# A hybrid decoder trunk on one core: the front and the RG-LRU gates in another order

## The chip, the cores and the metric

The kernel runs on one NeuronCore of a Trainium2 chip. TensorE does the matrix products, VectorE, ScalarE and GpSimd the elementwise work, and the SyncE queue most of the transfers. The traces call them PE, DVE, ACT, POOL and SP. The metric is the device time of one execution in microseconds (us); lower is better.

## The reference, cut to what matters

Two decoder layers over one sequence of 1024 tokens with 1024 features. Layer 0 joins native sparse attention with a second head group whose keys an indexer chooses: for each query, the 256 keys with the highest score. Layer 1 joins an RG-LRU (a width-4 convolution and a gated linear recurrence) with an mLSTM. Around each stand an RMSNorm, a gated side input and residual adds.

```python
hn = rmsnorm(x, norm_g[i])
# layer 0, the indexer: 4 heads of 64
idx_score = einsum('bqh,bqhs->bqs', wi, relu(einsum('bqhd,bsd->bqhs', qi, b_ki)))
_, sel_b = lax.top_k(where(key_pos <= t, idx_score, NEG), 256)
# layer 1, the RG-LRU: 8 blocks of 64
xc = causal_dwconv(x, conv_w, conv_b)
r  = sigmoid(einsum('bsgi,gij->bsgj', xb, wa) + ba)
ig = sigmoid(einsum('bsgi,gij->bsgj', xb, wx) + bx)
a  = exp(-8 * r * softplus(-lam))
h  = scan(a, sqrt(1 - a*a) * (ig * xc))
```

## The kernel before

A program in a tile language whose scheduler sets the order of instructions on each engine, except where a call goes through `Pinned`, which keeps the written order among the pinned calls of that engine.

Products are made in three passes (`mm3`): weights and activations are split into a high part (a ScalarE copy) and a low part (the rest, a subtraction on VectorE or GpSimd), and high × high, high × low and low × high are summed. The helper is `split`; in the trace its two lines are L119 (ScalarE) and L120 (VectorE or GpSimd).

*Front.* `x` is loaded in two halves of 512 tokens, eight tiles of 128 features (index `k`) each. `scaled` (L170, L171) multiplies by the norm's weights and splits, `square_sum` (L127, L130) sums squares, and `norms` turns the sum into 1/rms through a matmul (`ps_ss`, L139), a root, small VectorE steps and a broadcasting matmul (`ps_rs`, L160). The weights `wb` of the token-major projection are loaded beside `x` and split to `wbx` (k 0 to 5) and `wb` (k 6 and 7). For each of eight tiles of 128 tokens, 24 matmuls of 348 columns (8 k by three passes) make `ps_tok`. Tiles 0 to 3 are of half 0, 4 to 7 of half 1.

*Indexer.* `proj` (three passes over 8 k and two halves, 48 matmuls of 512 columns) makes the index queries and keys from chunks `wa[0]` to `wa[2]`. Then for query tiles 2 to 7 and four heads `ps_idx` goes through a ScalarE `relu` and a VectorE multiply-add (L363, L365) into `xall`.

*Search.* The 256th score of each query is found bit by bit, 31 steps. In each, VectorE makes `cand`, VectorE and ScalarE count (ScalarE into `junka`), and VectorE decides (`keep`, `pre`). Meanwhile TensorE makes sixteen projections (chunks 7 to 22), whose weights are loaded two chunks ahead by `fetched` (two loads from GpSimd's queue, then two `part` calls: ScalarE's `wh`, GpSimd's `wl`). A round is one chunk with two or three search steps. Each result goes through VectorE (`qz`). After the last round VectorE chooses the keys, makes `kc` and `blk`, and TensorE goes on with `ps_hid` (L542).

*RG-LRU.* For each of four chunks: a projection, its convolution (`conv`: VectorE `cin`, ScalarE, three VectorE steps into `lru`), a split to `xh` and `xl`, 12 gate matmuls (`ps_g`) with their sigmoids and the scan, and two more projections (chunks 4+c and 8+c, the mLSTM's q and k) whose convolutions end in `qk`. Then the mLSTM starts with `ps_S` (L1146).

Of the kernel before, what the change touches and what calls it, by code (L numbers as in the profile page):

```python
# [20 lines left out]
KT = 8  # L21
# [19 lines left out]
def rd(ap):  # L41
    return ap.bitcast(F32)
# [15 lines left out]
def trunk_kernel(ctx: ExitStack, tc: tile.TileContext, a, out):  # L58
    nc = tc.nc
    T, V, A, G = nc.tensor, nc.vector, nc.scalar, nc.gpsimd  # L60

    const = ctx.enter_context(tc.tile_pool(name="const", bufs=1))
    wq = nc.gpsimd
# [6 lines left out]
    def tmp(dt=F32, name="tmp", shape=(128, 512)):  # L70
        return tmpp.tile(list(shape), dt, name=name, tag="tmp")
# [4 lines left out]
    def mm1(name="mm1"):  # L76
        return psum.tile([128, 512], F32, name=name, tag="m1", bufs=3)

    def mmn(name):
        return psum.tile([128, 512], F32, name=name, tag="n1", bufs=1)  # L80
# [14 lines left out]
    rel = enter("rel", bufs=4)  # L95
    bigp = enter("big", bufs=7)
    wts, stage = enter("wts", bufs=3), 3
# [3 lines left out]
    def big(dt=F32, name="big", shape=(128, 1024)):  # L101
        return bigp.tile(list(shape), dt, name=name, tag="big")
# [7 lines left out]
    gn = const.tile([128, 3, KT], F32, name="gn")  # L110
# [7 lines left out]
    def split(h, l, src, eng=V):  # L118
        A.activation(h, src, AF.Copy)  # L119
        eng.tensor_tensor(l, src, rd(h), op=OP.subtract)  # L120
# [3 lines left out]
    def square_sum(x, acc):  # L124

        sq = tmp(name="sq")[:, :x.shape[1]]
        A.activation(sq, x, AF.Square)  # L127
        if acc is None:
            return sq
        V.tensor_tensor(sq, acc, sq, OP.add)  # L130
        return sq
# [36 lines left out]
    def scaled(x, g, k, h, l):  # L168

        A.activation(h, x, AF.Copy, scale=gn[:, g, k:k + 1])  # L170
        V.scalar_tensor_tensor(l, x, gn[:, g, k:k + 1], rd(h), op0=OP.mult, op1=OP.subtract)  # L171

    def norms(acc, cols, rows, i, table=False, later=0):
        c = rstd(acc, table)
        V.tensor_copy(cols[:, i * 4:i * 4 + 4], c)
        with tc.high_priority(offset=-later):
            A.activation(rows[:, HALF[i]], along(c), AF.Copy)
# [18 lines left out]
    def proj(src, X, nk=KT, w=None):  # L196
        w = w or weights(src, (nk, 128))
        ps = mm2("ps_proj")
        for c, sl in enumerate(HALF):
            for k in range(nk):  # L200
                mm3(ps[:, sl], *w[k], *X[c][k], k == 0, k == nk - 1)
        return ps
# [15 lines left out]
    def stack_q(ps, dst):  # L218
        for sl, t in times_norm(ps):
            for e in range(2):  # L220
                own, oth = slice(e * 64, e * 64 + 64), slice(64 - e * 64, 128 - e * 64)
                A.activation(dst[e][own, sl], t[own], AF.Copy)
                V.tensor_tensor(dst[e][oth, sl], t[own], rd(dst[e][own, sl]), OP.subtract)
# [8 lines left out]
    def stack_hl(t, own, k):  # L232
        oth = slice(64 - own.start, 128 - own.start)
        A.activation(k[own], t[own], AF.Copy)
        V.tensor_tensor(k[oth], t[own], rd(k[own]), OP.subtract)
# [6 lines left out]
    wb = []  # L242
# [4 lines left out]
    xin, win = [], []  # L247
# [19 lines left out]
    load_wb(big(name="wb"), 2)  # L267
    for k in range(0, KT, 2):
        load_x(1, k)
    for i in range(2):  # L270
        for k in range(KT):
            if i == 0:
                b = wbx[:, k * 696:k * 696 + 696] if k < 6 else big(F32R, "wb")
                wb.append((b[:, :348], b[:, 348:696]))
                split(*wb[k], win[k], G)
            scaled(xin[4 * i + k // 2][:, k % 2], 0, k, *X[i][k])
        acc = None
        for k in range(KT):
            acc = square_sum(xin[4 * i + k // 2][:, k % 2], acc)
        norms([acc], ncol, nrow, i, True)  # L280


    tok = l0.tile([128, NT, 348], F32, name="tok")
# [48 lines left out]
    qi = []  # L332
    for c in range(2):
        q2 = pair(n=("qi", "qi"))
        stack_q(proj(a["wa"][c], X), q2)
        qi += q2
    ps = proj(a["wa"][2], X)
    ki, kb = pair(), key()
    for sl, t in times_norm(ps):
        stack_k(t, lo, ki[0][:, sl], ki[1][:, sl])  # L340
        stack_hl(t, hi, kb[:, sl])


    xall = xp.tile([128, 4224], F32, name="xall", tag="x")
# [3 lines left out]
    for t in range(2, NT):  # L348
        n = 128 * (t + 1)
        xs[t] = xall[:, 64 * t * (t + 1) - 384:64 * t * (t + 1) - 384 + n]  # L350
        ms[t] = mall[:, 64 * t * (t + 1) - 384:64 * t * (t + 1) - 384 + n]
        for h in range(4):
            for c in range(0, n, 512):
                m = min(512, n - c)
                ps = mm1("ps_idx")
                for i in range(2):
                    T.matmul(ps[:, :m], qi[h][:, t * 128:(t + 1) * 128], ki[i][:, c:c + m], start=i == 0, stop=i == 1)
                x = xs[t][:, c:c + m]
                e = V
                r = rel.tile([128, 512], F32, name="relu", tag="relu")  # L360
                A.activation(r[:, :m], ps[:, :m], AF.Relu)
                if h == 0:
                    e.tensor_scalar(x, r[:, :m], wi[:, t, 0:1], None, op0=OP.mult)  # L363
                else:
                    e.scalar_tensor_tensor(x, r[:, :m], wi[:, t, h:h + 1], x, op0=OP.mult, op1=OP.add)  # L365
        V.tensor_tensor(xs[t][:, n - 128:], xs[t][:, n - 128:], cst0[:, C_CM - C_W:C_CM - C_W + 128], OP.add)


# [20 lines left out]
    junka = xp.tile([128, 1024], mybir.dt.int8, name="junka")  # L389
    bigc = const.tile([128, 1], F32, name="bigc")  # L390
    V.memset(bigc, BIG)
    PV, PA = Pinned(tc, V), Pinned(tc, A)

    def count(x, thresh, op, dst):
        PV.tensor_scalar(junk[:, :x.shape[1]], x, thresh, None, op0=op, op1=OP.add, accum_out=dst)
# [47 lines left out]
            mm3(ps, *w[k], *X[i][k], k == 0, k == KT - 1)  # L443
        V.tensor_tensor(out, ps, nrow[:, HALF[i]], OP.mult)

    def fetched(c):

        wh, wl = (wts.tile([128, 1024], F32R, name=n, tag=n) for n in ("wh", "wl"))
        parts = []
        for i in range(2):  # L450
            sl = slice(i * 512, i * 512 + 512)
            w = wts.tile([128, 512], F32, name="w", tag="w", bufs=stage)
            wq.dma_start(w.rearrange("p (a b) -> p a b", b=128), a["wa"][c][:, i * 4:i * 4 + 4])

            def part(w=w, sl=sl):
                PA.activation(wh[:, sl], w, AF.Copy)
                G.tensor_tensor(wl[:, sl], w, rd(wh[:, sl]), op=OP.subtract)  # L457
            parts.append(part)
        return [(wh[:, k * 128:k * 128 + 128], wl[:, k * 128:k * 128 + 128]) for k in range(KT)], parts

    def q_done(c, t):
        q2 = pair(n=("qst", "qst"))
        PA.activation(q2[0], t, AF.Copy)
# [8 lines left out]
        count(xs[t], 0.0, OP.is_ge, cnt[:, t - 2:t - 1])  # L472
    PV.tensor_scalar(pre, cnt, 255.5, -1.0, op0=OP.is_lt, op1=OP.mult)
    bits = list(range(30, -1, -1))
    chunks = list(range(7, 23)) + [3, 4, 6, 5]
    ends = [[2], [7], [6], [5], [4, 3]]
    got = [fetched(chunks[0]), fetched(chunks[1])]
    for _, parts in got:
        for f in parts:
            f()  # L480
    todo = []
    for n, c in enumerate(chunks[:16]):
        ps = proj(None, X, w=got[n][0])
# [80 lines left out]
    def first_keys(w, dst):  # L564
        ps, t = mm2("ps_kw")[:, :512], small.tile([128, 512], F32, name="kwp", tag="bt")
        half_proj(ps, w, 0, t)
        keys_of_groups(t, dst, HALF[0])

    def prefetch(c):
        w, parts = fetched(c)  # L570
        for f in parts:
            f()
        return w

    ps = proj(None, X, w=got[16][0])
    wkw = prefetch(6)
# [518 lines left out]
    for c in range(4):  # L1095

        ps = proj(a["ra"][c], X)
        late = []
        for half, sl in enumerate(HALF):
            conv(ps, c, half, x[:, sl])  # L1100
            xh, xl = rec(F32R, "xh"), rec(F32R, "xl")
            split(xh, xl, x[:, sl])
            pg = [mm1("ps_g"), mm1("ps_g")]
            for i in range(2):
                mm3(pg[i], *gws[i * 4 + c], xh, xl, True, True)
            A.activation(r[:, sl], pg[0], AF.Sigmoid, bias=vec[:, 0, c:c + 1])
            late.append(pg[1])
        for half, sl in enumerate(HALF):
            A.activation(ig[:, sl], late[half], AF.Tanh, scale=0.5, bias=vec[:, 1, c:c + 1])
            V.scalar_tensor_tensor(x[:, sl], ig[:, sl], 1.0, x[:, sl], op0=OP.add, op1=OP.mult)  # L1110
        h = hs[c]
        A.activation(ig, r, AF.Tanh, scale=s8[:, c:c + 1])
        A.activation(r, r, AF.Exp, scale=s8[:, c:c + 1])
        A.activation(h, r, AF.Square)
        V.scalar_tensor_tensor(h, h, 1.0, ig, op0=OP.add, op1=OP.mult)
        A.activation(h, h, AF.Sqrt, scale=-0.25)
        V.tensor_tensor(x, x, h, OP.mult)
        V.tensor_tensor_scan(h, r, x, 0.0, op0=OP.mult, op1=OP.add)
        v = wide(h1, (128, 2, S), F32, "qk")
        for i in range(2):  # L1120
            ps = proj(a["ra"][4 + 4 * i + c], X)
            for half, sl in enumerate(HALF):
                y = conv(ps, 4 + 4 * i + c, half, tmp(name="conv"))
                o = v[:, i, sl]
                A.activation(o, y, AF.Tanh, scale=0.5)
                V.scalar_tensor_tensor(o, o, 1.0, y, op0=OP.add, op1=OP.mult)
            qk[4 * i + c] = v[:, i]
# [203 lines left out]
```

## Time and profile before

| | |
|---|---|
| Three runs | 1558.91, 1560.05, 1555.63 us (median 1558.91) |
| The profiled execution | 1555.86 us; its span from first to last instruction is 1553.8 |
| TensorE busy | 1485.8 us (96%), mean granted clock 0.983 |
| VectorE, ScalarE, GpSimd busy | 1004.5 (65%), 799.8 (51%), 507.2 us (33%) |

A busy TensorE isn't one at its peak: its matmuls are pipelined and their shown ends overlap the next starts, so its pace is read from the distance between starts. "Granted clock" is the share of 2.4 GHz that the chip granted TensorE.

### The profile page before, as it was taken

How to read it: one execution, taken by the hardware profiler on the slowest of the kernel's cores; microseconds unless marked ns; L12 is line 12 of the kernel's file. 1: busy time of each engine (PE TensorE's matmuls, PEld its weight loads, DVE VectorE, ACT ScalarE, POOL GpSimd, SP SyncE). 2: the span in 40 equal slices, each digit the busy share in tenths (PEclk: the TensorE clock that was granted, in tenths of full speed). 3: DMA queues.
4: the chain of work that ended last, by engine and by line, in shares of the span. 5: the costliest groups of instructions: out<-in, count | busy, mean ns of one | idle time of the engine just before them, and what ended most of it. 6: DMA issues, size and time to landing. Idle time of an engine off the chain costs nothing.

```text
span 1553.8 us, 23978 instructions
## 1 busy us (share of the span) xinstructions
PE 1485.8 (96%) x8608; PEld 1226.2 (79%) x8608; DVE 1004.5 (65%) x2464; ACT 799.8 (51%) x1667; POOL 507.2 (33%) x506
## 2 busy tenths in 40 slices
PE   6999999998899999999999999999999999999996
PEld 5866888876677888888888789877777888788785
DVE  6269888975679888886234555287776654434456
ACT  6357878325678888777223335356654432223311
POOL 4204552312344453443232412022211122223636
PEclk9999999999999999999999999999999999999998
DMA  5402552255332121200323322011110021222203
GB/s 184 113 9 79 140 141 88 109 169 140 96 82 63 43 68 36 55 23 2 123 89 100 107 79 81 14 42 41 48 34 28 28 81 43 70 93 82 81 1 109
DMA packets 78088, 117.23 MB, mean 75 GB/s; under 512 B 7616, under 2 KB 43073, under 8 KB 77969
## 3 DMA queue, kind: packets, MB, share of 16 engines
q1 hardware_dynamic: 71360, 99.42, 21.1%
q0 software_dynamic: 3952, 12.62, 2.6%
q10 hardware_dynamic: 2656, 3.66, 1.0%
q8 instruction: 68, 1.11, 0.3%
q14 instruction: 52, 0.42, 0.1%
HBM read 94.83 MB, written 24.13 MB: 77 GB/s over the span
## 4 chain that ended last, share of the span: by engine, by line
PE 63%; DVE 17%; ACT 10%; issue 5%; POOL 2%; DMA 2%; SPq 0%; DVEq 0%; ACTq 0%; POOLq 0%
PE ps_proj L192 9%; PE ps_proj L193 9%; PE ps_proj L194 9%; PE ps_s L614 5%; PE ps_o L654 5%; ACT junka L53 5%; PE ps_pt L641 4%; PE ps_gate L192 3%; PE ps_gate L193 3%; PE ps_gate L194 3%; DVE L L622 3%; DVE tk L53 2%; DVE qz L53 1%; DVE conv L1082 1%; DVE lru L1082 1%
## 5 line engine op out<-in xcount | busy, mean ns | idle before, releaser
L120 POOL TENSOR_TENSOR wl<-w,wh 128x512 fp32r<-128x512 f32 (+1 forms) x110 | 155.7, 1432 | 463.3 <-ACT wh L119 445.5
L119 ACT ACTIVATE wh<-w 128x512 fp32r<-128x512 f32 (+1 forms) x110 | 64.8, 620 | 206.3 <-PE ps_proj L193 166.5
L626 ACT ACTIVATE L<-L,st 128x640 f32<-128x640 f32 (+7 forms) x192 | 143.1, 746 | 33.9 <-DVE st L622 26.2
L192 PE MATMUL ps_proj<-x1n,wh 128*128 128x512 f32 x384 | 152.0, 396 | 0.0
L614 PE MATMUL ps_s<-key,q 128*128 128x256 f32 (+3 forms) x576 | 150.5, 368 | 1.2 <-DVE st L622 0.6
L194 PE MATMUL ps_proj<-x1n,wl 128*128 128x512 f32 x384 | 151.4, 394 | 0.0
L193 PE MATMUL ps_proj<-x1n,wh 128*128 128x512 f32 x384 | 151.1, 394 | 0.0
L643 ACT ACTIVATE pt<-ps_pt 128x512 f32<-128x512 f32 (+3 forms) x288 | 124.4, 465 | 37.2 <-PE ps_pt L641 27.1
L192 PE MATMUL ps_proj<-x,wh 128*128 128x512 f32 x336 | 133.5, 397 | 1.8 <-ACT wh L53 1.8
L193 PE MATMUL ps_proj<-x,wh 128*128 128x512 f32 x336 | 134.3, 400 | 0.0
L194 PE MATMUL ps_proj<-x,wl 128*128 128x512 f32 x336 | 132.6, 395 | 1.7 <-POOL wl L457 1.7
L641 PE MATMUL ps_pt<-cst,L 128*128 128x128 f32 x816 | 125.6, 277 | 5.3 <-DVE L L631 4.3
L654 PE MATMUL ps_o<-pt,tok 128*64 128x128 f32 x1632 | 121.9, 281 | 0.6 <-ACT pt L643 0.6
L614 PEld LDWEIGHTS ps_s<-key,q 128*128 128x128 f32 x576 | 94.8, 193 | 24.3 <-issue 10.4
L641 PEld LDWEIGHTS ps_pt<-cst,L 128*128 128x128 f32 x816 | 95.3, 141 | 18.6 <-issue 5.5
L654 PEld LDWEIGHTS ps_o<-pt,tok 128*64 128x64 f32 x1632 | 91.9, 137 | 22.8 <-issue 18.5
L457 POOL TENSOR_TENSOR wl<-w,wh 128x512 fp32r<-128x512 f32 x40 | 54.2, 1363 | 149.4 <-ACT wh L53 149.3
L53 ACT ACTIVATE junka<-xall,cand 128x384 int8<-128x384 f32 (+2 forms) x93 | 83.6, 899 | 25.3 <-DVE cand L53 23.3
L193 PE MATMUL ps_proj<-y,wh 128*128 128x512 f32 x240 | 93.5, 389 | 0.8 <-DVE y L120 0.8
L192 PE MATMUL ps_proj<-y,wh 128*128 128x512 f32 x240 | 93.5, 389 | 0.1
L194 PE MATMUL ps_proj<-y,wl 128*128 128x512 f32 x240 | 93.4, 389 | 0.0
L53 DVE TENSOR_SCALAR_CACHE_REDUCE junk<-xall,cand 128x512 bf16<-128x512 f32 (+2 forms) x93 | 85.9, 924 | 3.3
(426 smaller groups left out, 3635.2 us busy)
## 6 DMA issues: line engine op xcount, KB each, us to landing
q<-qd SPq DMA_DIRECT2D x64, 256.0 KB, 4.1
w<-in_ra_dram SPq DMA_DIRECT2D x48, 256.0 KB, 2.6
w<-in_wa_dram POOLq DMA_DIRECT2D x46, 256.0 KB, 3.0
qd<-qst SPq DMA_DIRECT2D x32, 256.0 KB, 3.2
w<-in_wo_dram SPq DMA_DIRECT2D x32, 256.0 KB, 2.8
w<-in_gatew_dram SPq DMA_DIRECT2D x32, 256.0 KB, 2.9
x<-in_x_dram SPq DMA_DIRECT2D x8, 512.0 KB, 9.5
zd<-qz SPq DMA_DIRECT2D x8, 512.0 KB, 2.6
```

The costliest lines, as they stand in the source:

```text
L53: return self.tc.keep_in_program_order(getattr(self.eng, name)(*args, **kw))
L119: A.activation(h, src, AF.Copy)
L120: eng.tensor_tensor(l, src, rd(h), op=OP.subtract)
L192: T.matmul(ps, wh, xh, start=first, stop=False)
L193: T.matmul(ps, wh, xl, start=False, stop=False)
L194: T.matmul(ps, wl, xh, start=False, stop=last)
L457: G.tensor_tensor(wl[:, sl], w, rd(wh[:, sl]), op=OP.subtract)
L614: T.matmul(s[:, :m], q[:, i, h, :], keys[:, k0 + c:k0 + c + m], start=i == 0, stop=i == 1)
L626: A.activation(L[:, :n], L[:, :n], AF.Exp, bias=prev, scale=-1.0, accum_out=st[:, 2:3])
L641: T.transpose(pt[:, i * 128:(i + 1) * 128], L[:, (b + i) * 128:(b + i + 1) * 128], ident)
L643: A.activation(p[:, :m * 128], pt[:, :m * 128], AF.Copy)
L654: T.matmul(O[(h % 2) * 64:(h % 2) * 64 + 64, c * 128:c * 128 + 128], tok[:, d["k0"] // 128 + i, vi * 64:vi * 64 + 64], ps[i], start=False, ...
```

## The change

Three edits. In the front, TensorE begins with 14 products on a tile of zeros; half 0 is scaled and `wb` is split first, in a pinned order of ScalarE, VectorE and GpSimd, and squares come after that, those of half 0 between the scaling of half 1, those of half 1 last. The weights of the three index projections are fetched and split with pinned calls too, and the first two chunks of the search are fetched before the scores and split between them, one `part` after each of tiles 2 to 5. In the RG-LRU the next projection (chunk 4+c) is written ahead of the first half's gates.

```diff
-    for i in range(2):
-        for k in range(KT):
-            if i == 0:
-                b = wbx[:, k * 696:k * 696 + 696] if k < 6 else big(F32R, "wb")
-                wb.append((b[:, :348], b[:, 348:696]))
-                split(*wb[k], win[k], G)
-            scaled(xin[4 * i + k // 2][:, k % 2], 0, k, *X[i][k])
-        acc = None
-        for k in range(KT):
-            acc = square_sum(xin[4 * i + k // 2][:, k % 2], acc)
-        norms([acc], ncol, nrow, i, True)
+    idle = rel.tile([128, 512], BF, name="idle", tag="relu")
+    V.memset(idle, 0.0)
+    ps = mmn("ps_idle")
+    for _ in range(WARM):
+        T.matmul(ps, idle[:, :128], idle, start=True, stop=True)
+    PV, PA, PG = Pinned(tc, V), Pinned(tc, A), Pinned(tc, G)
...
+    def scale_tile(i, k):
+        h, l = X[i][k]
+        PA.activation(h, part(i, k), AF.Copy, scale=gn[:, 0, k:k + 1])
+        PV.scalar_tensor_tensor(l, part(i, k), gn[:, 0, k:k + 1], rd(h), op0=OP.mult, op1=OP.subtract)
+
+    def square(i, k, acc):
+        sq = tmp(name="sq")
+        PA.activation(sq, part(i, k), AF.Square)
+        if acc is not None:
+            PV.tensor_tensor(sq, acc, sq, OP.add)
+        return sq
+
+    for k in range(KT):
+        b = wbx[:, k * 696:k * 696 + 696] if k < 6 else big(F32R, "wb")
+        wb.append((b[:, :348], b[:, 348:696]))
+        PA.activation(wb[k][0], win[k], AF.Copy)
+        PG.tensor_tensor(wb[k][1], win[k], rd(wb[k][0]), op=OP.subtract)
+        scale_tile(0, k)
+    acc = None
+    for k in range(KT):
+        acc = square(0, k, acc)
+        scale_tile(1, k)
+    norms([acc], ncol, nrow, 0, True)
+    acc = None
+    for k in range(KT):
+        acc = square(1, k, acc)
+    norms([acc], ncol, nrow, 1, True)
...
+            PG.dma_start(w.rearrange("p (a b) -> p a b", b=128), a["wa"][c][:, i * 4:i * 4 + 4])
+
+            def part(w=w, sl=sl):
+                PA.activation(wh[:, sl], w, AF.Copy)
+                PG.tensor_tensor(wl[:, sl], w, rd(wh[:, sl]), op=OP.subtract)
...
+    wi3 = [prefetch(c) for c in range(3)]
...
-        stack_q(proj(a["wa"][c], X), q2)
+        stack_q(proj(None, X, w=wi3[c]), q2)
...
-    ps = proj(a["wa"][2], X)
+    ps = proj(None, X, w=wi3[2])
...
+    chunks = list(range(7, 23)) + [3, 4, 6, 5]
+    got = [fetched(chunks[0])]
+    ready = got[0][1][:]
...
+        if ready:
+            ready.pop(0)()
+            if not ready and len(got) == 1:
+                got.append(fetched(chunks[1]))
+                ready = got[1][1][:]
...
-    got = [fetched(chunks[0]), fetched(chunks[1])]
-    for _, parts in got:
-        for f in parts:
-            f()
...
+            if half == 0:
+                ahead = proj(a["ra"][4 + c], X)
...
-            ps = proj(a["ra"][4 + 4 * i + c], X)
+            ps = proj(a["ra"][8 + c], X) if i else ahead
```

On ScalarE in the front (high parts `x_102` to `x_105` are half 0, `x_106` and on half 1), before:

```order
L170 ACTIVATE x_103<-x,gn 128x512 x2
L119 ACTIVATE wbx<-wb 128x348 x2
L127 ACTIVATE sq<-x 128x512
L170 ACTIVATE x_104<-x,gn 128x512 x2
L119 ACTIVATE wbx<-wb 128x348 x2
L127 ACTIVATE sq<-x 128x512
L170 ACTIVATE x_105<-x,gn 128x512 x2
L127 ACTIVATE sq<-x 128x512 x4
L170 ACTIVATE x_106<-x,gn 128x512 x2
L119 ACTIVATE wb<-wb 128x348 x2
```

And of the change, from the fourth weight on (a pinned call's line is L54):

```order
L54 ACTIVATE wbx<-wb 128x348
L54 ACTIVATE x_103<-x,gn 128x512
L54 ACTIVATE wbx<-wb 128x348
L54 ACTIVATE x_104<-x,gn 128x512
L54 ACTIVATE wbx<-wb 128x348
L54 ACTIVATE x_104<-x,gn 128x512
L54 ACTIVATE wb<-wb 128x348
L54 ACTIVATE x_105<-x,gn 128x512
L54 ACTIVATE wb<-wb 128x348
L54 ACTIVATE x_105<-x,gn 128x512
L54 ACTIVATE sq<-x 128x512
L54 ACTIVATE x_106<-x,gn 128x512
```

The last two weight copies (`wb`, k 6 and 7) no longer stand behind six squares and two copies of half 1.

On GpSimd in the search, one round before (`DMA` issues one half of a chunk's load, `wl` is a half's low part, `qst` that of a query result):

```order
L464 TENSOR_TENSOR qst<-qz,qst 128x1024
L457 TENSOR_TENSOR wl<-w,wh 128x512
L453 DMA w<-in_wa_dram 128x512
L457 TENSOR_TENSOR wl<-w,wh 128x512
L453 DMA w<-in_wa_dram 128x512
```

And of the change:

```order
L506 TENSOR_TENSOR qst<-qz,qst 128x1024
L54 TENSOR_TENSOR wl<-w,wh 128x512 x2
L54 DMA w<-in_wa_dram 128x512 x2
L506 TENSOR_TENSOR qst<-qz,qst 128x1024
L54 TENSOR_TENSOR wl<-w,wh 128x512 x2
```

The first load of a chunk is issued one low part later, together with the second.

On TensorE at the second RG-LRU chunk's gates, before (row numbers count a kernel's rows on the engine; of the next projection's 48 matmuls 23 stand ahead of the first gate matmul):

```order
3576 L192 MATMUL ps_proj<-x1n,wh 128x512
3577 L193 MATMUL ps_proj<-x1n,wh 128x512
3578 L192 MATMUL ps_g<-xh,gws 128x512 x2
3579 L194 MATMUL ps_proj<-x1n,wl 128x512
3580 L193 MATMUL ps_g<-xl,gws 128x512
```

And of the change, where all 48 stand ahead:

```order
3623 L193 MATMUL ps_proj<-x1n,wh 128x512
3624 L194 MATMUL ps_proj<-x1n,wh 128x512
3625 L195 MATMUL ps_proj<-x1n,wl 128x512
3626 L193 MATMUL ps_g<-xh,gws 128x512
3627 L194 MATMUL ps_g<-xl,gws 128x512
```

The gates moved behind the whole projection of chunk 4+c.

## Rows read from the trace of the kernel before

**Rows 1.** The page, part 4: the chain that ended last, by engine.

```profile
PE 63%; DVE 17%; ACT 10%; issue 5%; POOL 2%; DMA 2%; SPq 0%; DVEq 0%; ACTq 0%; POOLq 0%
```

**Rows 2.** Busy time by window: length, engines (instructions), PE clock, DMA share, GB/s.

```profile
20.00:30.00 10.00, 7.01 (x27) 6.73 (x28) 8.60 (x17) 5.97 (x13) 2.25 (x2) 0.67 0.14 52
...
110.00:120.00 10.00, 9.98 (x40) 5.71 (x39) 10.00 (x23) 9.16 (x21) 0.00 (x0) 1.00 0.00 0
```

**Rows 3.** Groups of TensorE's instructions, 0 to 62 us: busy, mean, idle before.

```profile
L192 PE MATMUL ps_tok<-wbx,x 128*128 128x348 f32 x48 | 17.9, 377 | 8.4 <-ACT wbx L119 8.4
...
L192 PE MATMUL ps_tok<-wb,x 128*128 128x348 f32 x16 | 5.8, 361 | 0.6 <-ACT wb L119 0.6
L139 PE MATMUL ps_ss<-ones,sq 128*128 128x1 f32 x16 | 2.8, 297 | 2.8 <-DVE sq L130 2.8
L160 PE MATMUL ps_rs<-cst,rs 128*128 128x128 f32 x16 | 2.8, 333 | 2.9 <-DVE rs L153 2.9
```

**Rows 4.** Timeline of TensorE in the front: start, duration, instruction.

```profile
18.62 0.49 PE L193 MATMUL ps_tok<-wbx,x 128*128 128x348 f32 x1
18.91 0.49 PE L194 MATMUL ps_tok<-wbx,x 128*128 128x348 f32 x1
...
60.72 0.33 PE L192 MATMUL ps_tok<-wb,x 128*128 128x348 f32 x1
60.88 0.32 PE L193 MATMUL ps_tok<-wb,x 128*128 128x348 f32 x1
...
61.95 0.48 PE L192 MATMUL ps_proj<-x,wh 128*128 128x512 f32 x1
```

**Rows 5.** Timeline of ScalarE in the front.

```profile
11.37 0.88 ACT L119 ACTIVATE wbx<-wb 128x348 fp32r<-128x348 f32 x2 [0.30 <-DMA wb<-in_wb_dram]
...
19.71 0.86 ACT L119 ACTIVATE wb<-wb 128x348 fp32r<-128x348 f32 x2
```

**Rows 6.** Timelines of VectorE and GpSimd in the front.

```profile
13.41 2.76 DVE L171 SCALAR_TENSOR_TENSOR x<-x,gn,x 128x512 fp32r<-128x512 f32 x2
...
28.58 0.74 DVE L171 SCALAR_TENSOR_TENSOR x<-x,gn,x 128x512 fp32r<-128x512 f32 x1
...
14.45 2.50 POOL L120 TENSOR_TENSOR wbx<-wb,wbx 128x348 fp32r<-128x348 f32 x2 [0.17 <-ACT wbx L119]
```

**Rows 7.** Timelines of VectorE and GpSimd where the scores end.

```profile
119.70 0.28 DVE L366 TENSOR_TENSOR xall<-xall,cst 128x128 f32<-128x128 f32 x1
...
120.30 4.06 DVE L365 SCALAR_TENSOR_TENSOR xall<-relu,tok,xall 128x512 f32<-128x512 f32 x6
...
124.75 0.88 DVE L366 TENSOR_TENSOR xall<-xall,cst 128x128 f32<-128x128 f32 x1
...
123.14 3.62 POOL L457 TENSOR_TENSOR wl<-w,wh 128x512 fp32r<-128x512 f32 x2 [70.16 <-ACT wh L53]
...
127.29 1.29 POOL L457 TENSOR_TENSOR wl<-w,wh 128x512 fp32r<-128x512 f32 x1
```

**Rows 8.** Search: timelines of TensorE, ScalarE, GpSimd; the page's DMA issues.

```profile
329.36 7.17 PE L542 MATMUL ps_hid<-w,blk 128*128 128x256 f32 x32 [0.88 <-DVE blk L526]
...
180.02 0.62 ACT L53 ACTIVATE wh<-w 128x512 fp32r<-128x512 f32 x1
...
176.29 0.56 POOL L453 DMA_DIRECT2D w<-in_wa_dram  x1 [0.30 <-POOL wl L457]
...
w<-in_wa_dram POOLq DMA_DIRECT2D x46, 256.0 KB, 3.0
```

**Rows 9.** RG-LRU: TensorE's waits (us, times, longest), its timeline at chunk 1.

```profile
PE ps_g L192 <- ACT xh L119: 6.4, 4, 3.2
PE ps_S L1146 <- DVE qk L1126: 1.8, 1, 1.8
...
1054.19 1.22 PE L192 MATMUL ps_g<-xh,gws 128*128 128x512 f32 x2 [3.21 <-ACT xh L119]
...
1058.83 0.40 PE L192 MATMUL ps_proj<-x1n,wh 128*128 128x512 f32 x1
```

More of the change, by code (lines that the diff above doesn't have):

```diff
@@ L26 @@
 STEPS = (2, 3)
+WARM = 14
 LOAD, PREP = 1, 5
@@ new lines, in trunk_kernel @@
+    V.memset(idle, 0.0)
[3 more added lines that the diff above has]
+    PV, PA, PG = Pinned(tc, V), Pinned(tc, A), Pinned(tc, G)
+    part = lambda i, k: xin[4 * i + k // 2][:, k % 2]
+    def scale_tile(i, k):
[8 more added lines that the diff above has]
+        return sq
@@ new lines, in trunk_kernel, with fetched @@
+    norms([acc], ncol, nrow, 1, True)
+    def fetched(c):
+        wh, wl = (wts.tile([128, 1024], F32R, name=n, tag=n) for n in ("wh", "wl"))
+        parts = []
+        for i in range(2):
+            sl = slice(i * 512, i * 512 + 512)
+            w = wts.tile([128, 512], F32, name="w", tag="w", bufs=stage)
+            PG.dma_start(w.rearrange("p (a b) -> p a b", b=128), a["wa"][c][:, i * 4:i * 4 + 4])
+            def part(w=w, sl=sl):
+                PA.activation(wh[:, sl], w, AF.Copy)
+                PG.tensor_tensor(wl[:, sl], w, rd(wh[:, sl]), op=OP.subtract)
+            parts.append(part)
+        return [(wh[:, k * 128:k * 128 + 128], wl[:, k * 128:k * 128 + 128]) for k in range(KT)], parts
@@ L283, in trunk_kernel, with prefetch @@
+    def prefetch(c):
+        w, parts = fetched(c)
+        for f in parts:
+            f()
+        return w
+    wi3 = [prefetch(c) for c in range(3)]
     tok = l0.tile([128, NT, 348], F32, name="tok")
@@ L360, in trunk_kernel @@
                 r = rel.tile([128, 512], F32, name="relu", tag="relu")
-                A.activation(r[:, :m], ps[:, :m], AF.Relu)
+                PA.activation(r[:, :m], ps[:, :m], AF.Relu)
                 if h == 0:
@@ L391, in trunk_kernel @@
     V.memset(bigc, BIG)
-    PV, PA = Pinned(tc, V), Pinned(tc, A)
     def count(x, thresh, op, dst):
@@ L444, in half_proj @@
         V.tensor_tensor(out, ps, nrow[:, HALF[i]], OP.mult)
[L446 to L459, printed above, removed]
     def q_done(c, t):
@@ L474, in trunk_kernel @@
     bits = list(range(30, -1, -1))
-    chunks = list(range(7, 23)) + [3, 4, 6, 5]
     ends = [[2], [7], [6], [5], [4, 3]]
-    got = [fetched(chunks[0]), fetched(chunks[1])]
-    for _, parts in got:
-        for f in parts:
-            f()
     todo = []
@@ L567, in first_keys @@
         keys_of_groups(t, dst, HALF[0])
[L569 to L573, printed above, removed]
     ps = proj(None, X, w=got[16][0])
```

## The prediction

> **What bounds the kernel now.** I read the chain that ended last first: TensorE holds 63% of it, VectorE 17%, ScalarE 10% [rows 1]. So time is won where TensorE stands still or runs at its lower clock, or where a VectorE or ScalarE chain ends last. The stretches that the change touches show four such places.
>
> The front (0 to 62 us). The groups of the token matmuls say who keeps TensorE waiting: 8.4 us for ScalarE's first six weight copies (the wait at the very start is in it), 0.6 for the last two, 2.8 before `ps_ss`, 2.9 before `ps_rs` [rows 3]. Its pace shows in the starts of neighbouring 348-column matmuls: 0.29 us apart at 18.6, 0.16 at 60.7, and the first projection begins at 61.95 [rows 4]. After the gap before `ps_ss` the granted clock of 20 to 30 us is 0.67, a mix of the two levels, 1.2 and 2.4 GHz [rows 2]. All 192 token matmuls at 0.16 are 30.7 us; the stage takes twice that.
>
> The scores (100 to 124 us). VectorE is busy 10.00 of 10.00 us from 110 to 120 [rows 2]: it is the bound, and TensorE's matmuls between its operations are free.
>
> The search (124 to 329 us). `ps_hid` at 329.36 waited 0.88 us for VectorE's `blk` [rows 8]. So the projections don't end this stage, the VectorE and ScalarE chain through the bit search does, and a front that is shorter pays here only by moving that chain.
>
> The RG-LRU (1000 to 1160 us). Four waits before `ps_g` for ScalarE's `xh` make 6.4 us, the longest 3.2, and `ps_S` waits 1.8 once for `qk` [rows 9].
>
> **The change, part by part.** *Front.* With squares and half-1 scaling no longer ahead of half 0's weights, the third weight copy still starts at 11.37, since it waits for its load [rows 5]. Six k are left from there. GpSimd's two low parts took 2.50 us, VectorE's two beside them 2.76, 1.38 each [rows 6]; at the slower of the two, six take 8.3 us and half 0 is ready at 19.7. Before, the last two weight copies only began then, at 19.71 [rows 5]. Half 1 is VectorE's: eight low parts and seven additions at 0.74 (no GpSimd beside them [rows 6]; the additions have the same width) are 11.1 us, to 30.8. TensorE does tiles 0, 1 and 4 to 6 meanwhile (120 matmuls: 19 us at 0.16, behind the data). Left are 72 matmuls, 11.5 us, to 42.3; the sums and the row broadcast, 2.8 + 2.8 busy [rows 3], to 47.9; and from the last token matmul to the first projection 1.1 as now (60.88 to 61.95 [rows 4]): 49.0 for 61.95, a gain of **12.9**. Bounds: if the 2.8 of the broadcasts lie beside tokens, 15.7. If both norm chains again leave a gap with the lower level behind it: a mean of 0.67 over 10 us [rows 2] is 6.6 us at half of the full clock, at 6.6 × (1 − 0.16/0.29) = 3.0 each, so 6.9 remain. The 14 products on zeros cost, by columns from the lower pace, 14 × 0.29 × 512/348 = 6.0 us, inside the 8.4 in which TensorE waits for first copies [rows 3]. I give them no gain and no cost of their own. The three projections' weights are now split on the same engines in a pinned order; the first copy stands behind the second half's row norm, some 30 matmuls before the tokens end, 4.8 us for a copy and a 1.29 split, so nothing is due late.
>
> *Scores.* Four copies go to ScalarE, which has room, and four GpSimd splits of 1.29 us beside a VectorE that is the bound. What a collision costs the trace shows two ways. In the front VectorE paid: 1.38 for 0.74, so 0.65 a split. At 120 to 124 us it paid little, six operations in 4.06 us or 0.68 each, the last of them beside GpSimd, and GpSimd paid, 3.62 us for two splits that are 1.29 alone [rows 7]. So 0 to 1.29 a split, and I take the front's, as the operands are of the same kind: **+2.6** (0 to 5.2). The Trainium skill (SBUF — State Buffer, section "SBUF: two separate sides") says that VectorE with two SBUF inputs and GpSimd take a shared port pair for a whole instruction, the other being fully blocked; by that the four would cost the 5.2, and the sum would be 2.6 us higher. The trace agrees that they collide, but not on a full stop of VectorE each time.
>
> *Search start.* The same splits leave 123 to 131 us, where a VectorE addition took 0.88 for 0.28 [rows 7]: **−0.6**. The projection matmuls that now stand among the score matmuls give TensorE a longer lead, but the chain through `blk` ends the stage, so the lead becomes a longer wait before `ps_hid`. After the 3.2 us gap in the RG-LRU 13 matmuls took 1054.19 to 1058.83, 4.64 us, where 0.2285 each would be 2.97: a long gap costs 1.7 of lower clock behind it [rows 9]. I add **+1.7** (0 if the gap stays short, 3.4 if two of them open).
>
> *Loads in the search.* GpSimd now issues a chunk's two loads together behind its second split, so the first goes out one split later. In the two-step rounds (8 of 16) that is as at 176.29, and landing takes 3.0, so 179.3; the copy that needs it starts at 180.02 [rows 8]. Margin 0.7: I take 0, and see the rivals.
>
> *RG-LRU.* A whole projection, 48 matmuls or 11 us at 0.2285, stands between a projection and its gates, where about half did. The waits of 1.0 to 3.2 are covered with 2 us to spare: 6.4 plus the 1.7 of lower clock [rows 9] are **−8.1**. VectorE's gate chain starts about 4 us later in each chunk; behind the last chunk 34 in place of 23 other matmuls stand before the waiting `ps_S`, so that wait should stay near its 1.8. Bounds −4 (it grows by a gap and its clock) and −9.
>
> Sum: −12.9 + 2.6 − 0.6 + 1.7 − 8.1 = −17.3. The profiled run took 1555.86, the lowest but one of four; the median of the others is 3.05 higher, and I go from half way, 1557.4: **1540**.
>
> **Rivals.** *A, the lower clock stays in the front*: both norm chains still stop TensorE, since sums, root and broadcast depend on each other whatever the order. For it: both did [rows 3]. Against: VectorE's scaling no longer stands between the small steps. 6.9 for 12.9: 1546.
>
> *B, the splits stop VectorE in full* in the scores, 5.2 for 2.6: 1543. For it: 3.62 for two splits shows that one side can lose most of an instruction. Against: both sides shared the loss so far.
>
> *C, the gates are late anyway*: VectorE and ScalarE now have the next projection's convolution in front of or among the gate steps, and the wait goes to the next chunk's gates or to `ps_S`. Against it: eleven us of projection matmuls again stand between, before each chunk's gates. Without the 8.1: 1548.
>
> *D, it comes to nothing*: A with B's price and C's loss, −6.9 + 5.2 − 0.6 + 1.7 = −0.6: 1557.
>
> *E, slower*: the later load makes ScalarE's copy wait in every two-step round, with the counting passes of the search chain queued behind it, on which VectorE's `keep` waits. It decides where landing takes over 3.7 us; eight rounds eat the gain of 17.3 at 5.9 us and make it slower by 0.3% at 6.5. At 6.8: 1540 + 8 × 3.1 = 1565. For it: the margin is 0.7 us. Against: 3.0 is the median of 46 such loads [rows 8], and half the rounds have three steps.
>
> **How the numbers follow.** Forecast 0.55, A 0.16, B 0.12, C 0.08, D 0.05, E 0.04. A measurement here tells about 0.3%, 4.7 us, from no change. Faster is the first four, 0.91; same D, 0.05; slower E, 0.04. Range: with the front's 15.7 and neither the scores' nor the clock's cost 1533, and a little below for the base, 1532; upwards C and a mix of A and B, 1550. That leaves out D and E.
>
> **What would show it.** First projection near 49 us, with no long wait before the seventh and eighth weight; last `ps_idx` at most 24 us after its first; the search with the same step time, no ScalarE wait for a load; a wait of some 5 us before `ps_hid`; no wait over 0.5 us before `ps_g`, and `ps_S` not much above 1.8. The prediction is wrong if the search steps lengthen, if the front's gain isn't found again at `ps_hid`, or if new waits appear in the RG-LRU.

## The result, and the profile after

The changed kernel takes 1540.63 us (median of four runs, 1539.68 to 1541.62) against 1559.48 before (four runs): ratio 0.9876, 95% interval 0.9856 to 0.9897. The forecast was 1540. The profiled run took 1540.62 against 1555.86, 15.2 us less, so the terms below have to make 15.2 (the sum of the prediction was 17.3). The times of one kernel spread by 2 to 11 us here, so stages are compared by their traces.

| from the timelines, us | before | after | gained so far |
|---|---|---|---|
| first projection matmul | 61.95 | 50.52 | 11.4 |
| VectorE's first score operation | 101.48 | 90.05 | 11.4 |
| end of its last score multiply-add | 124.36 | 116.35 | 8.0 |
| first `keep` of the search | 134.90 | 125.40 | 9.5 |
| last `keep` | 271.14 | 259.20 | 11.9 |
| first `ps_hid` | 329.36 | 317.29 | 12.1 |
| first `ps_kw` | 336.18 | 326.21 | 10.0 |
| first `ps_m`, ahead of the RG-LRU | 995.85 | 984.94 | 10.9 |
| last four `ps_n` of the mLSTM | 1245.20 | 1229.60 | 15.6 |

The chain of the changed kernel by engine (the page, part 4), which answers to [rows 1]: TensorE's share has grown, VectorE's and ScalarE's have shrunk.

```profile
PE 67%; DVE 15%; ACT 9%; issue 5%; POOL 3%; DMA 2%; SPq 0%; DVEq 0%; POOLq 0%; ACTq 0%
```

The windows (columns as in [rows 2]): VectorE is still full in the scores, now at 100 to 110, and the 0.67 of 20 to 30 us is gone. The lower level now lies at 10 to 20, while TensorE mostly waits for data; in the kernel before the token matmuls started 0.29 us apart at 18.6 too [rows 4].

```profile
10.00:20.00 10.00, 9.35 (x32) 7.25 (x33) 9.27 (x9) 9.83 (x19) 8.26 (x9) 0.66 1.06 383
20.00:30.00 10.00, 10.00 (x66) 10.00 (x64) 8.07 (x13) 5.05 (x9) 0.00 (x0) 1.00 0.07 25
...
100.00:110.00 10.00, 9.33 (x41) 6.34 (x40) 10.00 (x18) 8.16 (x19) 5.08 (x4) 1.00 0.10 39
```

TensorE's groups in the front (as [rows 3]): the waits of 2.8 and 2.9 for the two norm chains are 0.9 and 0.3. The 8.4 us for weight copies are 2.0 for copies of `x`, but that is no gain: 6.7 of the 8.4 were the wait from the start of the span, in which the products on zeros now stand, and the first token matmul begins at 6.90 in place of 6.70.

```profile
L193 PE MATMUL ps_tok<-wbx,x 128*128 128x348 f32 x48 | 16.2, 345 | 2.0 <-ACT x L54 2.0
...
L161 PE MATMUL ps_rs<-cst,rs 128*128 128x128 f32 x16 | 2.2, 279 | 0.3 <-DVE tb L360 0.3
L140 PE MATMUL ps_ss<-ones,sq 128*128 128x1 f32 x16 | 2.0, 246 | 0.9 <-DVE sq L54 0.9
```

The scores on VectorE and GpSimd (timelines, as [rows 7]). The operations that grow most are the ones with a single tensor input: `TENSOR_SCALAR` of 512 columns takes 1.23 in place of 0.48, of 384 columns 1.45 in place of 0.41, beside a GpSimd split that itself takes up to 2.71. Six multiply-adds of the same tile lose 1.0 (3.89; 2.86 before). The addition that follows the counting takes 0.28 again, since no split is left there.

```profile
95.69 1.23 DVE L416 TENSOR_SCALAR xall<-relu,tok 128x512 f32<-128x512 f32 x1 [0.21 <-ACT relu L54]
...
97.90 3.89 DVE L418 SCALAR_TENSOR_TENSOR xall<-relu,tok,xall 128x512 f32<-128x512 f32 x6
...
106.35 1.45 DVE L416 TENSOR_SCALAR xall<-relu,tok 128x384 f32<-128x384 f32 x1
...
116.74 0.28 DVE L424 TENSOR_TENSOR xall<-xall,cst 128x128 f32<-128x128 f32 x1
...
104.87 2.71 POOL L54 TENSOR_TENSOR wl<-w,wh 128x512 fp32r<-128x512 f32 x1 [3.23 <-ACT wh L54]
```

Before `ps_hid` (as [rows 8]) stands the wait that the longer lead of TensorE turns into, and behind it the lower level: 0.79 over ten us.

```profile
317.29 2.93 PE L579 MATMUL ps_hid<-w,blk 128*128 128x256 f32 x6 [4.83 <-DVE blk L563]
```

The window of the ten us from there (columns as in [rows 2]):

```profile
317.29:327.29 10.00, 10.00 (x36) 8.46 (x37) 8.32 (x10) 2.49 (x3) 1.03 (x1) 0.79 0.23 70
```

In the RG-LRU (TensorE's waits, as [rows 9], and below them two timelines at the last chunk) the waits for `xh` are gone, but three of 1.0 us have come, ahead of the tenth of twelve gate matmuls, for a sigmoid (L1139) that stands behind two weight copies and a table load.

```profile
PE ps_g L193 <- ACT lru L1139: 3.0, 3, 1.0
PE ps_S L1179 <- DVE qk L1159: 1.7, 1, 1.7
```

The timelines of ScalarE and TensorE there:

```profile
1118.63 1.15 ACT L120 ACTIVATE wh<-w 128x512 fp32r<-128x512 f32 x2 [3.09 <-PE ps_proj L194]
1119.81 1.28 ACT L1139 ACT_TABLE_LOAD   x1
1121.10 0.69 ACT L1139 ACTIVATE lru<-ps_g,vec 128x512 f32<-128x512 f32 x1
...
1121.84 0.50 PE L193 MATMUL ps_g<-xh,gws 128*128 128x512 f32 x1 [0.99 <-ACT lru L1139]
```

### The profile page after: what moved, and what is told of

The parts are those of the page before. It is cut to its first block, busy times and chain, and to the rows that moved or that the text cites. A ratio compares the mean times of both kernels' runs of the same rounds, so it can differ in the third digit from the quotient of the medians.

```text
span 1538.8 us, 24004 instructions
## 1 busy us (share of the span) xinstructions
PE 1482.5 (96%) x8622; PEld 1223.3 (79%) x8622; DVE 997.8 (65%) x2465; ACT 799.6 (52%) x1667; POOL 509.6 (33%) x506
## 4 chain that ended last, share of the span: by engine, by line
PE 67%; DVE 15%; ACT 9%; issue 5%; POOL 3%; DMA 2%; SPq 0%; DVEq 0%; POOLq 0%; ACTq 0%
PE ps_proj L194 10%; PE ps_proj L193 10%; PE ps_proj L195 10%; ACT junka L54 5%; PE ps_o L685 5%; PE ps_s L645 5%; PE ps_pt L672 4%; PE ps_gate L193 3%; DVE L L653 3%; PE ps_gate L194 3%; PE ps_gate L195 3%; DVE tk L54 2%; DVE qz L54 1%; DVE junk L54 1%; PE ps_hid L579 1%
## 5 line engine op out<-in xcount | busy, mean ns | idle before, releaser
L121 POOL TENSOR_TENSOR wl<-w,wh 128x512 fp32r<-128x512 f32 (+1 forms) x104 | 152.2, 1482 | 434.7 <-ACT wh L120 434.2
L120 ACT ACTIVATE wh<-w 128x512 fp32r<-128x512 f32 (+1 forms) x104 | 61.1, 621 | 224.3 <-PE ps_proj L194 182.3
L54 POOL TENSOR_TENSOR wl<-w,wh 128x512 fp32r<-128x512 f32 x46 | 62.4, 1361 | 169.8 <-ACT wh L54 167.1
L672 PEld LDWEIGHTS ps_pt<-cst,L 128*128 128x128 f32 x816 | 95.2, 141 | 18.6 <-issue 5.5
L54 ACT ACTIVATE junka<-xall,cand 128x384 int8<-128x384 f32 (+2 forms) x93 | 83.6, 899 | 29.2 <-DVE cand L54 27.1
L54 DVE TENSOR_SCALAR_CACHE_REDUCE junk<-xall,cand 128x512 bf16<-128x512 f32 (+2 forms) x93 | 85.9, 924 | 3.3
```

The costliest lines, as they stand in the source:

```text
L54: return self.tc.keep_in_program_order(getattr(self.eng, name)(*args, **kw))
L672: T.transpose(pt[:, i * 128:(i + 1) * 128], L[:, (b + i) * 128:(b + i + 1) * 128], ident)
```

## The experiments

### The new front alone

The kernel before with the new front block (products on zeros, pinned order), and nothing else of the change: the projections' weights are again loaded and split where the scheduler puts them.

> The kernel before with the new front alone (products on zeros, pinned order of scaling, weights and squares); scores, search and RG-LRU as before. Theory 1, the stages add: the first projection begins near 50.5 us as in the changed kernel, the scores keep their 23 us, the search its old steps, ps_hid starts 11.4 us earlier than before (near 318), and the run is about 11 us faster (ratio 0.993). Rival, the front pays only because later waits move with it: ps_hid gains under 6 us and the run less than that.

1554.86 us against 1559.01, ratio 0.9973 (0.9959 to 0.9987). Theory 1 missed, and the rival's number (under 6 us at `ps_hid`) came for another reason: the gain does arrive at `ps_hid` in full, but there is only 2.2 us of it at the first projection (59.74), and 2.1 at `ps_hid` (327.28). The timelines of VectorE and GpSimd show where it went.

```profile
27.82 1.78 DVE L54 SCALAR_TENSOR_TENSOR x<-x,gn,x 128x512 fp32r<-128x512 f32 x1
29.52 1.77 DVE L54 TENSOR_TENSOR sq<-sq 128x512 f32<-128x512 f32 x1
31.22 1.90 DVE L54 SCALAR_TENSOR_TENSOR x<-x,gn,x 128x512 fp32r<-128x512 f32 x1
...
42.15 4.84 DVE L54 TENSOR_TENSOR sq<-sq 128x512 f32<-128x512 f32 x4 [0.51 <-ACT sq L54]
...
27.25 3.49 POOL L121 TENSOR_TENSOR wl<-w,wh 128x512 fp32r<-128x512 f32 x2 [4.97 <-ACT wh L120]
...
31.26 1.29 POOL L121 TENSOR_TENSOR wl<-w,wh 128x512 fp32r<-128x512 f32 x1
...
43.49 2.96 POOL L121 TENSOR_TENSOR wl<-w,wh 128x512 fp32r<-128x512 f32 x2 [9.92 <-ACT wh L120]
```

The splits of the projections' weights (`wl`, 512 columns) run in the middle of VectorE's half-1 work, and operations of 0.68 and 0.74 us take 1.8. Half 1's last low part ends at 34.4 (28.1 in the changed kernel). The last four additions of its squares take 4.84 us beside two more splits (3.08 in the changed kernel), and TensorE waits 2.69 us for that second sum, until 47.05, with the lower level after it. Some 1.5 us more were lost at the start, where this run's third low part of `x` began at 12.1 (10.6 in the changed kernel).

### The old front with the pinned fetch

```diff
-    idle = ...; 14 products; scale_tile / square in pinned order
+    for i in range(2):   # the loop of the kernel before
+        ...split(*wb[k], win[k], G); scaled(...); square_sum(...); norms(...)
     wi3 = [prefetch(c) for c in range(3)]   # pinned, behind both norms
```

The rest is the changed kernel's.

> The changed kernel with the old front loop (no products on zeros, squares where the scheduler puts them), but with the pinned fetch of the three index projections' weights behind both norms. The front alone gave 2.2 us at the first projection, the whole change 11.4. Theory 2, most of the rest is that GpSimd's splits of the projections' weights no longer run beside VectorE's half-1 work: then the old loop with the pinned fetch loses its gap before ps_rs and the lower clock behind it (2.9 and some 1.5 to 3 us), and the first projection begins at 56 to 58 us, each half of the edit being worth some 5 us only with the other. Rival a, the fetch alone is the gain: 50 to 53 us. Rival b, it does nothing without the new order: 61 to 62 us.

The first projection begins at 54.05: 7.9 us gained by the pinned fetch with the old loop, more than theory 2 and less than rival a expected. No wait before `ps_rs` is left. The kernel's ten times spread from 1542.76 to 1553.45 (median 1550.75, ratio 0.9948, 0.9926 to 0.9969), so it was run again.

> The old front loop with the pinned fetch of the projections' weights once more, since its ten times spread over 10 us and its profiled run was the fastest. If the front is not what varies, the first projection begins within 1 us of the 54.05 seen; if it is, some 3 to 7 us later.

55.84, in a run of 1545.08: 1.8 later than in the first run, neither within 1 nor 3 to 7 later. The two lines:

```profile
54.05 0.48 PE L193 MATMUL ps_proj<-x,wh 128*128 128x512 f32 x1
...
55.84 0.48 PE L193 MATMUL ps_proj<-x,wh 128*128 128x512 f32 x1
```

So at the first projection the new order alone is worth 2.2, the pinned fetch alone 6.1 to 7.9, and both 11.4 (9.3 to 11.6 in the other runs with both). These are good to 1 or 2 us only: the old front itself, profiled once more with the gates alone changed (below), reaches the first projection at 60.53 and not 61.95. From there the new order gives 0.8 and the pinned fetch 4.7 to 6.5, so the fetch is the larger part on either base.

What the fetch takes away shows in the kernel before: three splits run beside small VectorE operations that stand in its queue among the steps of the second norm; a copy takes 1.14 us in place of 0.16 and a cast 1.71 in place of 0.17. The norm's later steps stand behind them, and TensorE's wait of 2.9 before `ps_rs` [rows 3] ends with the last of these steps.

```profile
38.76 1.14 DVE L310 COPY tbb<-tbp 32x16 bf16<-32x16 bf16 x1
...
40.00 1.71 DVE L309 CAST tbp<-tb 96x16 bf16<-96x16 f32 x1
...
37.34 2.53 POOL L120 TENSOR_TENSOR wl<-w,wh 128x512 fp32r<-128x512 f32 x2 [14.81 <-ACT wh L119]
...
40.39 1.28 POOL L120 TENSOR_TENSOR wl<-w,wh 128x512 fp32r<-128x512 f32 x1
```

The larger spread between runs lies behind the front. The attention, from about 350 to 730 us, whose code no edit touches, takes 368.5 to 375.4 us from its first `ps_s` to its last, and the difference is there within the first 75. It goes with TensorE's granted clock: from 350 to 420 us that is 0.93 in the two shortest (the front alone, and the work for the wait before `ps_hid`), 0.80 and 0.76 in the two longest (the splits after the scores, and the gates alone), and 0.85 to 0.90 in the others. Why the clock differs there stays open.

### The front without the products on zeros

```diff
-WARM = 14
+WARM = 0
```

> The changed kernel without the 14 products on zeros. Theory 1: they only lift the pace of the first dozen matmuls, which wait for loads anyway; TensorE falls to the lower level near 11 us in either, so the first projection begins within 1 us of 50.5. Rival, they hold the clock through the front: without them the lower level lasts some us longer and the first projection begins 3 us or more later.

1540.24 us, ratio 0.988 (0.9854 to 0.9906); the first projection begins at 51.26, 0.7 later, and in a second run of the changed kernel with the products it began at 51.84. Theory 1 holds for the time, not for the clock: without the products the token matmuls never start less than 0.29 us apart until 19.6, so there is no higher level to fall from near 11; with them TensorE is at the higher level until 11 us and again from 17.8. What the products gain at the first projection is less than a front's own spread between runs.

### The splits after the scores, as before

```diff
-    got = [fetched(chunks[0])]; ready = ...   # one part after each of tiles 2 to 5
+    for c in chunks[:2]:                      # behind the scores
+        got.append(fetched(c)); both parts
```

> The changed kernel with the weights of the first two search chunks fetched and split after the scores, as before (still pinned). Theory 1: the four splits cost the scores 3.4 us, and their place at the search's start 1.5, so VectorE's scores take 22.8 us from first to last operation in place of 26.2, the counting passes behind them 1.5 more, and TensorE's wait before ps_hid, 4.8 in the changed kernel, shrinks to under 2 with no lower clock behind it: ps_hid about 2 us earlier, the run about 4 us faster than the changed kernel. Rival, the early weights are what carries the search: the first result comes late, the search's start loses over 4 us, and the run is slower than the changed kernel.

1543.25 us, ratio 0.9896 (0.9871 to 0.9921). The scores take 22.9 us from first to last operation and not 26.3, as expected, and TensorE doesn't wait before `ps_hid`. But the counting and the first step behind the scores take 2.7 us more, not 1.5, and `ps_hid` comes at 317.15, as in the changed kernel (317.29): what the splits cost the scores they cost the search's start too, but for some tenths. There `cand`, six elements wide, takes 1.22 us beside a split.

```profile
119.50 1.24 DVE L54 TENSOR_SCALAR pre<-cnt 128x6 int32<-128x6 f32 x1
120.78 1.22 DVE L54 TENSOR_SCALAR cand<-pre 128x6 int32<-128x6 int32 x1
...
119.43 2.54 POOL L54 TENSOR_TENSOR wl<-w,wh 128x512 fp32r<-128x512 f32 x2 [2.64 <-ACT wh L54]
```

The 2.2 us at `ps_kw` (323.98) that the missing wait and its lower clock give are lost in the attention behind it, where this run has the granted clock of 0.80 named above and the changed kernel 0.90. The run isn't faster: theory 1 hit the scores and the missing wait, and missed the time and what the splits cost behind the scores.

### The splits before the scores

```diff
+    got, qi = [], []
     for c in range(2):
...
         qi += q2
+        got.append(fetched(chunks[c]))
+        for f in got[c][1]:
+            f()
```

> The changed kernel with the splits of the first two search chunks' weights moved from the scores to the projections before them (right behind the first and second). Theory 1, it is the collision with the bound VectorE that costs: the scores' VectorE work takes 22.8 us again in place of 26.3, the search's start stays 1.5 us shorter than before, the first keep comes about 3.4 us earlier than in the changed kernel, ps_hid too, and the run is about 3 us faster than the changed kernel. Rival, the scores are longer because of projection matmuls in TensorE's order among them: they stay at 26 us.

1536.59 us, ratio 0.9864 (0.9836 to 0.9893). The scores take 22.1 us, though the projection matmuls still stand among them, and the first `keep` comes at 122.20, 3.2 earlier than in the changed kernel though its first projection began 1.0 later. So it is GpSimd beside a full VectorE that costs, and not TensorE's order. The operation that took 1.45 takes 0.42:

```profile
104.18 0.42 DVE L418 TENSOR_SCALAR xall<-relu,tok 128x384 f32<-128x384 f32 x1
104.51 3.66 DVE L420 SCALAR_TENSOR_TENSOR xall<-relu,tok,xall 128x512 f32<-128x512 f32 x6
```

### The search's loads left to the scheduler

```diff
-            got.append(fetched(chunks[n + 2]))       # GpSimd's calls pinned
+            got.append(fetched(chunks[n + 2], G))    # not pinned
```

> The changed kernel with GpSimd's loads and splits in the search's rounds left to the scheduler, as before (one load issued between two splits). Theory 1, the 2.4 us that the search gained come from the pinned order: splits back to back end 0.6 us sooner, and VectorE's cand no longer waits beside them. So four two-step rounds take 5.66 us again in place of 5.06, and the stretch from the first to the last keep 136.2 in place of 133.8. Rival, they come from the early weights or from TensorE's lead: 133.8 as in the changed kernel.

First to last `keep`: 136.2 us, and 133.8 in the changed kernel; one step in each of four rounds takes 5.63 to 5.66 again, where the changed kernel has 5.06 or 5.07. Theory 1 holds. The timelines of a two-step round of this kernel, VectorE's `cand` and GpSimd:

```profile
154.13 0.93 DVE L54 TENSOR_SCALAR cand<-pre 128x6 int32<-128x6 int32 x1
...
151.56 1.28 POOL L319 TENSOR_TENSOR wl<-w,wh 128x512 fp32r<-128x512 f32 x1
153.14 0.55 POOL L315 DMA_DIRECT2D w<-in_wa_dram  x1 [0.30 <-POOL wl L319]
153.72 1.30 POOL L319 TENSOR_TENSOR wl<-w,wh 128x512 fp32r<-128x512 f32 x1
```

And of the changed kernel, 1.3 us earlier: with no load between the splits the second starts sooner against `keep`, and `cand` takes 0.37. In the three rounds like it `cand` takes 0.25, 0.16 and 0.16 here, and 0.84, 0.75 and 0.75 in the kernel above.

```profile
152.84 0.37 DVE L54 TENSOR_SCALAR cand<-pre 128x6 int32<-128x6 int32 x1
...
150.27 1.29 POOL L54 TENSOR_TENSOR wl<-w,wh 128x512 fp32r<-128x512 f32 x1
151.88 1.29 POOL L54 TENSOR_TENSOR wl<-w,wh 128x512 fp32r<-128x512 f32 x1 [0.32 <-ACT wh L54]
153.12 1.09 POOL L54 DMA_DIRECT2D w<-in_wa_dram  x2
```

The three runs with the scheduler's order (before, the front alone, the gates alone) all have 136.2 to 136.3, those with the pinned order 133.8 to 133.9, one of them 134.6. That one (without the products on zeros) shows rival E's mechanism once: ScalarE waits 0.7 us for a load, and the step takes 5.23 in place of 4.41.

### The projection ahead of the gates alone

```diff
+            if half == 0:
+                ahead = proj(a["ra"][4 + c], X)
...
-            ps = proj(a["ra"][4 + 4 * i + c], X)
+            ps = proj(a["ra"][8 + c], X) if i else ahead
```

> The kernel before with the projection ahead of the gates alone. Theory 1: the four waits for xh (6.4 us) and the lower clock behind the longest go, three waits of about 1 us for a sigmoid come (4 gate products in 3 accumulator banks), so the RG-LRU is 4 to 6 us shorter and the run 0.997. Rival, the wait only moves (to ps_S, or to the next chunk's gates): under 2 us, ratio 0.999 to 1.000.

1553.27 us, ratio 0.9962 (0.994 to 0.9983). From `ps_m` to the last `ps_n` it takes 243.0 us where the kernel before takes 249.35: 6.3 gained, with three waits of 1.0 for the sigmoid and 1.7 at `ps_S`, as in the changed kernel. Theory 1 holds, a little above its bound. The profiled run of the changed kernel shows 244.7; the other runs with this edit show 243.0 to 243.1. What it has more is a stretch of lower clock (0.72 from 985 to 990 us, 1.00 in its second run), so the edit is worth 6.3 and that run shows 4.7 of it.

### A fourth bank for the gates

```diff
-            pg = [mm1("ps_g"), mm1("ps_g")]
+            pg = [mm1("ps_g"), mmn("ps_g") if half else mm1("ps_g")]
```

> The changed kernel with the fourth gate product of each RG-LRU chunk in a fourth accumulator bank. Theory 1: the three waits of 1.0 us behind the ninth gate matmul are for a bank that the first sigmoid frees, and that sigmoid stands behind a table load; with a fourth bank the three waits vanish, and the stretch from the first gates to ps_S is 3 us shorter. Rival, the gates wait for the sigmoid's engine in some other way (xh or the next projection's weights): the waits stay or move to another matmul.

The three waits vanish and `ps_S` comes 2.9 us sooner after the first gate, so they were for a bank. But the run isn't faster than the changed kernel's by more than its spread, 1539.68, ratio 0.988 (0.9843 to 0.9917). VectorE's chain to `qk` doesn't come sooner by as much, the wait at `ps_S` grows from 1.7 to 2.8, and behind it the clock falls, which it didn't behind 1.7. TensorE's wait:

```profile
PE ps_S L1179 <- DVE qk L1159: 2.8, 1, 2.8
```

And the window behind it:

```profile
1140.00:1150.00 10.00, 8.60 (x32) 7.14 (x32) 5.92 (x13) 2.48 (x8) 0.52 (x1) 0.66 0.00 0
```

From `ps_S` to the last `ps_n` it takes 87.7 us and the changed kernel 84.8: 2.9 won, 2.9 given back.

### Work for the wait before `ps_hid`

```diff
+    first_keys(wkw, kw)
     compress(0)
     blocks_of(1, ps)
-    first_keys(wkw, kw)
     compress(1)
```

> The changed kernel with the projection ps_kw (24 matmuls, 5.6 us) written ahead of ps_hid. Theory 1, the front's gain ends in a TensorE wait of 4.8 us before ps_hid, with 2 us of lower clock behind it: with work to do there the wait shrinks to about 1 (a bank that VectorE's kc frees), and the first score matmul ps_s comes 5 to 6 us earlier. Rival, VectorE's blk chain holds everything behind it: ps_hid comes no earlier, the second ps_hid waits in its place, and ps_s gains under 2 us.

1538.76 us, ratio 0.9875 (0.9837 to 0.9913). The 4.8 us are gone; the waits of this kernel from 300 to 345 us are:

```profile
PE ps_hidt L586 <- DVE hid L583: 2.0, 1, 2.0
PE ps_kw L193 <- DVE kc L553: 1.1, 1, 1.1
```

`ps_s` begins at 347.49, 3.5 us earlier, though `ps_hid` itself, now behind `ps_kw`, begins 1.8 later (319.07). That lies between the two expectations: `ps_hidt` now waits 2.0 for `hid`, since the matmuls that stood there have been moved.

### Both edits that gained, and the changed kernel beside them

> The changed kernel with both edits that gained: the first two search chunks' weights split behind the index projections, and ps_kw ahead of ps_hid. Theory 1, they add: the first keep 3 us earlier and the first ps_s another 3.5, so some 6 to 7 us less than the changed kernel, about 1533 to 1534 (ratio to before 0.983 to 0.984). Rival, they fill the same slack before ps_hid: 3 to 4 us less, 1536 to 1537.

> The changed kernel once more, on the chip and in the call of the kernel with both edits, to compare with it: about 1540.6 us, and the first projection within 1 us of 50.5, ps_hid within 1 us of 317.3.

Both together: 1534.27 us, ratio 0.9844 (0.9823 to 0.9865). The changed kernel beside it: 1540.25, ratio 0.9885 (0.9865 to 0.9905). The edits add: the first `keep` is 3.4 us earlier than in the changed kernel beside it (123.33, 126.70), the first `ps_s` 5.8 (346.37, 352.20), the run 6.0. This is the fastest version here. This second run of the changed kernel has its first projection at 51.84 and `ps_hid` at 318.59, each 1.3 later than the first and not within 1 as expected, so a front repeats within 1 to 2 us.

## Why the prediction was right

The time, 1540 for 1540.6, and the two largest terms held. That it came so close is partly luck. The sum, 17.3, is 2.1 above the 15.2 of the profiled run, and the base of 1557.4 is 1.5 above that run's 1555.86, which nearly cancels it; inside the sum, what the front and the RG-LRU fell short of (1.5 and 3.4) is partly made up by gains that weren't foreseen. Of its own signs two failed: new waits did appear in the RG-LRU, by which it had said that it would be wrong, and the last `ps_idx` comes 26.7 us after the first, not at most 24. Term by term, forecast, measured in the profiled run:

- **Front, −12.9, −11.4.** The size was nearly right, the reason for most of it wrong. The step that failed is that the projections' weights were given no gain ("nothing is due late"), and that the whole 12.9 were counted to the order of scaling and squares. That order alone gives 2.2, the pinned fetch of the projections' weights alone 6.1 to 7.9, each good to 1 or 2 us. What the prediction didn't see: before, their splits ran beside small VectorE operations among the second norm's steps (1.14 and 1.71 us, above), and without a pinned place they run beside half 1's work with the new order (1.8 us an operation in the front alone). The working took VectorE's 0.74 "no GpSimd beside them" for granted; with the new order it holds only because of the edit that it priced at nothing. In the sum, half 0 was ready sooner than 19.7 (its last low part ends at 18.6, and TensorE is at the higher level from 17.8), half 1 at 28.1 and not 30.8; but TensorE itself was then behind, and its last token matmul ends at 49.94.
- **Scores, +2.6, +3.4.** The mechanism is shown by the early and the late splits: 22.1 and 22.9 us without, 26.3 with them. A split costs 0.85, above the front's price of 0.65 and below the full stop of 1.29. Rival B's 5.2 did not come. The page SBUF — State Buffer of the Trainium skill (section "SBUF: two separate sides") has the later of the two fully blocked. The trace agrees in part: the 3.4 us lie below the 5.2 that the prediction worked out by it, and GpSimd's 2.71 for a split of 1.29 shows that in part of the collisions it was GpSimd that waited.
- **Search start, −0.6, −1.5.** Mis-sized: only one operation of that stretch was counted, and a second, `pre`, took 1.06 and takes 0.17.
- **Search, 0, −2.4.** Not foreseen. The later load, rival E's ground for a loss, is a gain: ScalarE waits for no load in this run, and the splits, now back to back, leave VectorE's `cand` 0.6 us shorter in each of four rounds. The step that failed asked only what the moved DMA delays, not what it had delayed.
- **Clock behind `ps_hid`, +1.7, +2.1.** As forecast, behind a wait of 4.8 ("some 5").
- **RG-LRU, −8.1, −4.7.** The waits for `xh` vanish as forecast, but three of 1.0 come for an accumulator bank, which the prediction didn't count, and 1.6 went to a lower clock that other runs don't show: the edit's own worth is 6.3. `ps_S` waits 1.7, as forecast, and rival C's loss isn't there.
- The rest, −0.9 between `ps_kw` and `ps_m`, lies in code that the change doesn't touch.

Measured: −11.4 + 3.4 − 1.5 − 2.4 + 2.1 − 0.9 − 4.7 = −15.4, for −15.2.

## What to carry to other kernels

Where VectorE is full, put GpSimd's elementwise work where VectorE has room, even if that is many microseconds earlier: here four splits moved from the scores to the projections gave 3 us, and six pinned behind the norms gave more than the new order of the front (4.7 to 7.9 us against 0.8 to 2.2). An edit that only fixes the order of an engine off the path is to be priced by whom its instructions stand beside, before and after. A gain that ends in a wait is spent there, and here a lower clock behind the wait was added: look for work to put into it (`ps_kw`, 3.5 us) before removing the next small wait, which with the fourth bank was worth nothing here.

## What the runs showed of the hardware

- Beside a GpSimd split VectorE's operations suffer unequally: a `TENSOR_SCALAR` of six elements takes 1.22 us in place of 0.17, one of 384 columns 1.45 in place of 0.41, while counting passes with an accumulator keep their time (`TENSOR_SCALAR_CACHE_REDUCE` of 512 columns 0.67 beside a split and without one).
- TensorE's clock: a wait of 1.7 us before `ps_S` had no lower level behind it in any profiled run, one of 2.8 at the same place had (0.66 over ten us, one run), as had 4.8 before `ps_hid` (0.79, and the lower level in all eight profiled runs with that wait). The length of a wait doesn't settle it alone: behind 0.9 us before `ps_ss` the ten us from 40 are at 1.00 in the changed kernel's first run and at 0.83 in its second. In the front TensorE fell to the lower level at about 11 us in spite of 14 products on zeros before it, while it worked on and off between waits for data, and rose near 17.8 when data came without gaps.
